# Tile 0 leaves the gating stage early, the last tile runs two chunks alone, and the weight stream waits for VectorE

## The chip, the cores and the metric

The kernel runs on one core of a Trainium2 chip. The metric is the device time of one execution, in microseconds (us). Before the change the median of three runs is 2240.0 us (2239.03 to 2240.32).

## The reference, cut to what matters

One step of a two-layer hybrid encoder runs over 1024 prompt rows and 32 sample rows of width 1024, all in fp32. Layer 0 mixes rows with spatial gating, layer 1 with trailing mean pooling. Each layer ends in a channel MLP with squared ReLU of width 4096. Conditioning (`mod`) is a product of a silu of `c` and a 1024 x 6144 weight per layer.

```python
mod = silu(c) @ w_ada[i] + b_ada[i]            # 6 vectors per request and layer
h = rmsnorm(x, g_norm[i, 0]) * (1 + sc1) + sh1
# layer 0: gating
z = gelu(h @ sgu_w_in); u, v = split(z, 2)
v = rmsnorm(v, g_v)                            # also an output, for the sample rows
s = einsum('gij,bnjgd->bnigd', w_s * mask, v) + b_s      # within chunks of 128 rows
mix = (u * s) @ sgu_w_out
# layer 1: mean over the last 2, 4, 8, 16 rows minus the row, a map per group, a scale
x = x + gt1 * rmsnorm(mix, g_norm[i, 1])
h = rmsnorm(x, g_norm[i, 2]) * (1 + sc2) + sh2
f = square(relu(h @ ffn_w_up[i])) @ ffn_w_down[i]
x = x + gt2 * rmsnorm(f, g_norm[i, 3])
```

## The kernel before

Activations lie transposed (features on partitions, rows on columns) in three token tiles: 384, 384 and 256 + 32 = 288 columns, called tiles 0, 1 and 2. To keep fp32 precision each operand of a large product is split in a high and a low part. `products` (L766) runs three matmuls per term: high x high (L771), low x high (L772) and high x low (L773).

**Weights.** Every weight arrives as pieces of 128 x 1024 fp32 (512 KB). SyncE's queue (SP) loads a piece into one of three `raw` buffers (L359), ScalarE (ACT) copies its high part `wh` (L367), and VectorE (DVE) subtracts to get the low part `wl`. Nearly all DVE work is recorded under line 79, so tiles tell it apart. Eight pairs of `wh` and `wl` are held at once. `w_finish` gives a pair back.

**One stream.** All loads stand in one list, `stream`, in a fixed order: weight pieces ("w"), conditioning pieces ("ada") and input rows ("x"). `weave` (L585) is called after each small unit of matmuls. It emits up to `streams` steps of the list (`stream_step`, L517) while a weight pair is free, and then pulls `fillers`, which are generators of residual, norm and output work, as long as a model of the time says that DVE is behind TensorE (`time["dve"] < time["pe"]`). `need_w` (L535) emits steps until the weight it is asked for is there. The order within each engine is thus fixed when the kernel is built.

**Conditioning.** From the v stage on, a conditioning piece is eight DVE operations on 128 x 256 each into an accumulator `aa` that has one buffer (`do_ada`, L429). Two pieces, so 16 operations, fill it. Then TensorE folds it with four small matmuls (`ada`, L453). After every fourth fold ACT copies the result (`adas`, L465) and TensorE transposes it (`adat`, L469). The folds go to a `deferred` list that the next step or `weave` empties.

**Stages of layer 0.** The v stage multiplies pieces p = 0..3 of `sgu_w_in` with nine row blocks (`v_mm`, L798 to L800; block 8, the sample rows, L790 and L791) and writes v to DRAM (`v_end`). The gating stage runs four pairs of groups, (0,1), (2,3), (4,5) and (6,7); for each pair `sgu_group` (L946) loads a 128 x 128 `w_s` per group and transposes it (`wsT`), and `sgu_item` (L958) then runs tiles 0, 1 and 2 in that order. An item has four "up" units (product `pu`, ACT Gelu L993, gating product `psp` L997, and DVE and ACT operations to `ush` and `usl`) and a "down" part (`po`), which is held back and emitted after the first up unit of the next item. After a tile's last item `mix_to_ffn` (L1138) becomes a filler: it takes the mixer's row norm (`pn_rs`, ACT reciprocal square root L675), adds the residual, takes the next norm (`pn_r`) and makes the FFN's input `hh` and `hl`.

**Passes.** The FFN runs as the list `passes` of (layer, chunk, tiles). A chunk is 512 of the 4096 hidden features and has eight weight pieces. In layer 0 chunks 0 and 1 run tile by tile, 2 and 3 over all three tiles, and 4 to 7 tile by tile; in layer 1 chunks 0 to 3 run tile by tile and 4 to 7 over all tiles. A pass over several tiles uses a loaded weight for all of them; a pass over one tile loads it again for the next.

**The end.** Tiles 0 and 1 go out through `to_out`, a filler: the final norm, 24 transposes `yT` (L1393), a copy `yo` (L1394) and a store (L1395) per tile. Tile 2 is last. While its final down products end, `scale_last` and `turn_last` (L1128, L1134) scale and transpose the result per feature block d. Then `last` (L1343) adds the squares, takes the norm per row (`pn_last`, `r_last`, then `ms_last`, `q_last`), applies it to the six 128 x 512 halves (`xlast`) and stores them (L1377).

Of the kernel before, what the change touches and what calls it, by code (L numbers as in the profile page):

```python
# [9 lines left out]
F32 = mybir.dt.float32  # L10
# [5 lines left out]
P = 128  # L16
D = 1024
# [17 lines left out]
def tile_stream_encoder_step(  # L35
# [84 lines left out]
    inv = const.tile([P, 16], F32, name="inv")  # L120
    epsT = const.tile([P, 1], F32, name="eps")
    nc.vector.memset(epsT, EPS * D / P)
    eps1 = const.tile([P, 1], F32, name="eps1")
    nc.vector.memset(eps1, EPS)
    for i in range(16):
        nc.vector.memset(inv[:, i : i + 1], 1.0 / (i + 1))

# [119 lines left out]
        for q in range(4):  # L247
            add_w(*v_item(p, q))

    def w_groups(gs):  # L250
        for g in gs:
            for k in range(2):
                f = 2 * g + k
                add_w(
                    ("u", g, k),
                    sgu_w_in[0][:, f * P : (f + 1) * P].rearrange("(k p) f -> p k f", p=P),
                    (8, P),
                )
        for q in range(2):
            for g in gs:  # L260
                add_w(
                    ("o", g, q),
                    sgu_w_out[0][g * 256 : (g + 1) * 256, q * 512 : (q + 1) * 512].rearrange(
                        "(k p) d -> p k d", p=P
                    ),
                    (2, 512),
                )
# [23 lines left out]
    passes += [(0, c, every) for c in range(2, 4)]  # L291
    passes += [(0, c, [t]) for t in every for c in range(4, 8)]
    passes += [(1, c, [t]) for t in every for c in range(4)]
    passes += [(1, c, every) for c in range(4, 8)]

    rest = []

# [20 lines left out]
        w_vpiece(p)  # L318
        some_ada(8)
    rest += [(1, j) for j in (*range(8, 16), *range(8), *range(16, 48))]  # L320
    groups = [(g, g + 1) for g in range(0, 8, 2)]
    for i, gs in enumerate(groups):
        w_groups(gs)
        if i < 3:
            some_ada((6, 8, 8)[i])
    wide = [n for n, (l, _, tiles) in enumerate(passes) if len(tiles) > 1]
    for n in range(len(passes)):
        w_chunk(n)
        if n in wide:
            some_ada(12 if passes[n][0] == 0 else 2)  # L330
    some_ada(99)

    worder = [s[1] for s in stream if s[0] == "w"]
# [1 line left out]
    wdone = set()  # L335
    raws = {}
    loads = {}
    state = {"issued": 0, "next": 0, "raw": 0}
    deferred = []

    def in_raw(k):
# [175 lines left out]
    def stream_step():  # L517
# [14 lines left out]
            state["raw"] -= 1  # L532
        issue()

    def need_w(key):  # L535
        while key not in witem:
            assert stream_ready(), key
            stream_step()
        return witem[key]
# [45 lines left out]
    def weave(streams=1):  # L585
        if streams:
            n = 0
            run_deferred()
            while n < streams and stream_ready():
                stream_step()  # L590
                n += 1
        while time["dve"] < time["pe"] and fillers:
            if not pull():
                break
# [27 lines left out]
    class Stat:  # L622

        def __init__(self, t, tag, split=True):
            self.t, self.tag, self.n, self.split = t, tag, ncol[t], split

        def square(self, k, src=None):

            if k == 0:
                self.sq = room("l", self.t, f"sq_{self.tag}")
            sq = self.sq
            w = 1 if src is None else 2
            act(
                out=sq[:, k, :] if w == 1 else sq[:, k : k + 2, :],
                in_=A(self.t, k) if w == 1 else src,
                func=AF.Square,
            )

            if w == 1:
                for j in [k - 1] if k < 7 else [6, 7]:
                    if j > 0:
                        tt(out=sq[:, 0, :], in0=sq[:, 0, :], in1=sq[:, j, :], op=ALU.add)
            else:
                for j in [k - 2] if k < 6 else [4, 6]:
                    if j > 0:
                        tt(out=sq[:, 0:2, :], in0=sq[:, 0:2, :], in1=sq[:, j : j + 2, :], op=ALU.add)
                if k == 6:
                    tt(out=sq[:, 0, :], in0=sq[:, 0, :], in1=sq[:, 1, :], op=ALU.add)  # L650
            if k + w == KB and self.split:
# [303 lines left out]
        nc.vector.memset(wt[64:P, 0:64], 0.0)  # L955
        return wt, bb

    def sgu_item(gs, t, mix, after):  # L958
        n = ncol[t]
        col0, npr, nsm = TILES[t]  # L960
        nch = npr // P
# [21 lines left out]
        def up(g, k):  # L983
            f = 2 * g + k
            if k == 0:
                inputs(g)
            vl, wr, bb = vls[g], wrs[g], mix[g][1]
            ps = ps_up(f"pu{g}_{t}_{k}")
            products(ps, n, up_terms(("u", g, k), t))
            if t == NT - 1:  # L990
                w_finish(("u", g, k))
            u = t_m(f"u{g}_{t}_{k}")
            act(out=u[:, :n], in_=ps[:, :n], func=AF.Gelu_apprx_tanh)  # L993
            sp = ps_up(f"psp{g}_{t}_{k}")
            tick(0.24 * nch + 0.2)
            for c in range(nch):
                mm(  # L997
                    sp[:, c * P : (c + 1) * P],
                    vl[:, c, k * P : (k + 1) * P],
                    wr[:, c * P : (c + 1) * P],  # L1000
                    start=True,
                    stop=True,
                )
# [29 lines left out]
            hid.append((a, b))  # L1033

        def down():
            for d in range(KB):
                ps = ps_dn(f"po{gs[0]}_{t}_{d}")
                terms = []
                for j, (a, b) in enumerate(hid):
                    wh, wl = need_w(("o", gs[j // 2], d // 4))  # L1040
                    o = (j % 2) * 512 + (d % 4) * P
                    terms.append((wh[:, o : o + P], wl[:, o : o + P], a[:, :n], b[:, :n]))
                products(ps, n, terms)
# [2 lines left out]
                    st = Stat(t, f"rs_{t}")  # L1046
                if after is not None:
                    st.square(d)
                if t == NT - 1 and d % 4 == 3:
                    for g in gs:  # L1050
                        w_finish(("o", g, d // 4))
                weave(d % 2)
            if after is not None:
                after(st)
# [8 lines left out]
    def ffn_item(p, t, after):  # L1063
# [17 lines left out]
        def down():  # L1081
            for d in range(KB):
# [11 lines left out]
                if after is not None:  # L1094
                    st.square(d)
                    if l == 1 and t == NT - 1:
                        scale_last(d)
                        if d > 0:
                            turn_last(d - 1)
                if last and d % 2 == 1:  # L1100
                    w_finish(("dn", p, d // 2))
# [59 lines left out]
    def to_ffn0(st):  # L1161
        fillers.append((f"ffn0_{st.t}", mix_to_ffn(st, 0)))

    for gs in groups:
        mix = {g: sgu_group(g) for g in gs}
        for t in range(NT):
            sgu_item(gs, t, mix, to_ffn0 if gs == groups[-1] else None)

    sgu_stack.close()
    late = pool("late")  # L1170
# [163 lines left out]
    def to_out(st):  # L1334
# [7 lines left out]

        def last():  # L1343

            turn_last(KB - 1)
            pn = ps_dn("pn_last")
            nb = len(LAST)
            for i, (c0, _, _) in enumerate(LAST):
                mm(
                    pn[:, 2 * i : 2 * i + 2],  # L1350
                    st.sq[:, 0, c0 : c0 + P],
                    ones[:, 0:2],
                    start=True,
                    stop=True,
                )
            sums = pn[:, : 2 * nb].rearrange("p (b c) -> p b c", c=2)[:, :, 0]
            ms, r, q = (t_st(f"{x}_last")[:, :nb] for x in ("ms", "r", "q"))
            act(out=r, in_=sums, func=AF.Abs_reciprocal_sqrt, bias=eps1, scale=1.0 / D)
            ts(ms, sums, 1.0 / D, EPS, op0=ALU.mult, op1=ALU.add)
            tt(out=q, in0=r, in1=r, op=ALU.mult)  # L1360
            stt(out=q, in0=q, scalar=-0.5, in1=ms, op0=ALU.mult, op1=ALU.mult)
            stt(out=r, in0=q, scalar=1.5, in1=r, op0=ALU.add, op1=ALU.mult)
            xt = last_ps["x"]
            dsts = [dst for _, _, dst in blocks]
# [82 lines left out]
```

## Time and profile before

| | |
|---|---|
| median of three runs | 2240.0 us |
| profiled execution: its own time | 2238.69 us |
| profiled execution: its span | 2236.9 us |
| TensorE busy | 98% |
| VectorE busy | 61% |
| ScalarE busy | 43% |
| 512 KB weight pieces of the FFN | 144 up, 144 down |
| conditioning pieces | 96 |

How to read the rows below. A row of the table by windows has the window, its length, the busy time and instruction count of TensorE (PE), its weight loads (PEld), DVE, ACT and GpSimd (POOL), then the TensorE clock that was granted (1.00 is full speed), the DMA engines' busy share and the GB/s. A row of the timeline has start, duration, engine, line, operation, output <- inputs, shapes, and in brackets the idle time before and what ended it. A row of the waits has the engine, what waited, what it waited for, then total us, times and longest. A group of the page has the line, operation and count, then busy time and mean ns of one. "SPq" is SyncE's DMA queue. Matmuls overlap, so a row's duration is longer than its spacing from the next.

### The profile page before, as it was taken

How to read it: one execution, taken by the hardware profiler on the slowest of the kernel's cores; microseconds unless marked ns; L12 is line 12 of the kernel's file. 1: busy time of each engine (PE TensorE's matmuls, PEld its weight loads, DVE VectorE, ACT ScalarE, POOL GpSimd, SP SyncE). 2: the span in 40 equal slices, each digit the busy share in tenths (PEclk: the TensorE clock that was granted, in tenths of full speed). 3: DMA queues.
4: the chain of work that ended last, by engine and by line, in shares of the span. 5: the costliest groups of instructions: out<-in, count | busy, mean ns of one | idle time of the engine just before them, and what ended most of it. 6: DMA issues, size and time to landing. Idle time of an engine off the chain costs nothing.

```text
span 2236.9 us, 33683 instructions
## 1 busy us (share of the span) xinstructions
PE 2197.3 (98%) x13478; PEld 2101.8 (94%) x13478; DVE 1371.4 (61%) x2609; ACT 957.5 (43%) x1645; POOL 0.7 (0%) x6
## 2 busy tenths in 40 slices
PE   7999799999999999999999999999999999999998
PEld 5777699999998999999999999999999999999998
DVE  4855735675568765766446869878765553424355
ACT  4633323121256654133435556666565542312334
POOL 0000000000000000000000000000000000000000
PEclk9999999999999999999999999999999999999998
DMA  8465613232235544333444546665454551202112
GB/s 298 149 226 164 206 53 116 79 126 88 78 104 184 171 132 142 104 123 109 132 125 131 166 156 201 184 189 163 145 166 135 152 155 45 93 10 85 57 50 95
DMA packets 344896, 295.67 MB, mean 132 GB/s; under 512 B 10178, under 2 KB 322954, under 8 KB 344740
## 3 DMA queue, kind: packets, MB, share of 16 engines
q1 hardware_dynamic: 344468, 293.43, 42.1%
q8 instruction: 105, 1.72, 0.3%
q14 instruction: 51, 0.42, 0.1%
q10 hardware_dynamic: 272, 0.10, 0.0%
HBM read 261.65 MB, written 31.84 MB: 131 GB/s over the span
## 4 chain that ended last, share of the span: by engine, by line
PE 91%; DMA 1%; DVE 1%; ACT 1%; issue 0%; DVEq 0%; SPq 0%; ACTq 0%
PE pf L771 11%; PE pf L772 11%; PE pf L773 11%; PE pg L771 11%; PE pg L772 11%; PE pg L773 11%; PE pu L771 3%; PE po L771 3%; PE po L772 3%; PE po L773 3%; PE pu L772 3%; PE pu L773 3%; PE pv L798 1%; PE pv L799 1%; PE pv L800 1%; PE pp L1310 1%
## 5 line engine op out<-in xcount | busy, mean ns | idle before, releaser
L771 PE MATMUL pf<-hh,wh_up 128*128 128x384 f32 (+1 forms) x1536 | 498.0, 324 | 1.2 <-ACT r L1075 1.0
L772 PE MATMUL pf<-hl,wh_up 128*128 128x384 f32 (+1 forms) x1536 | 497.0, 324 | 1.8 <-DVE hl L79 1.7
L771 PE MATMUL pg<-fh,wh_dn 128*128 128x384 f32 (+1 forms) x1536 | 498.3, 325 | 0.0
L773 PE MATMUL pf<-hh,wl_up 128*128 128x384 f32 (+1 forms) x1536 | 496.1, 323 | 0.0
L772 PE MATMUL pg<-fl,wh_dn 128*128 128x384 f32 (+1 forms) x1536 | 494.7, 322 | 0.0
L773 PE MATMUL pg<-fh,wl_dn 128*128 128x384 f32 (+1 forms) x1536 | 494.0, 322 | 0.0
L771 PEld LDWEIGHTS pf<-hh,wh_up 128*128 128x128 f32 x1536 | 288.6, 188 | 4.3 <-issue 2.0
L772 PEld LDWEIGHTS pf<-hl,wh_up 128*128 128x128 f32 x1536 | 288.7, 188 | 3.0 <-DVE hl L79 2.6
L771 PEld LDWEIGHTS pg<-fh,wh_dn 128*128 128x128 f32 x1536 | 288.4, 188 | 3.0 <-issue 1.2
L772 PEld LDWEIGHTS pg<-fl,wh_dn 128*128 128x128 f32 x1536 | 288.6, 188 | 0.7
L773 PEld LDWEIGHTS pg<-fh,wl_dn 128*128 128x128 f32 x1536 | 288.7, 188 | 0.0
L773 PEld LDWEIGHTS pf<-hh,wl_up 128*128 128x128 f32 x1536 | 288.6, 188 | 0.0
L367 ACT ACTIVATE wh_up<-raw 128x1024 fp32r<-128x1024 f32 x144 | 152.7, 1061 | 287.2 <-PE pf L772 230.8
L79 DVE TENSOR_TENSOR wl_up<-raw,wh_up 128x1024 fp32r<-128x1024 f32 x144 | 176.2, 1224 | 160.8 <-ACT wh_up L367 160.4
L79 DVE TENSOR_TENSOR acc<-acc,pg 128x384 f32<-128x384 f32 (+1 forms) x336 | 174.1, 519 | 159.8 <-PE pg L773 159.2
L367 ACT ACTIVATE wh_dn<-raw 128x1024 fp32r<-128x1024 f32 x144 | 152.7, 1061 | 206.2 <-PE pg L772 173.3
L79 DVE SCALAR_TENSOR_TENSOR aa<-raw,csil,aa 128x256 f32<-128x256 f32 x560 | 231.9, 478 | 2.4 <-DMA raw<-in_w_ada_dram 2.4
L79 DVE TENSOR_TENSOR wl_dn<-raw,wh_dn 128x1024 fp32r<-128x1024 f32 x144 | 176.2, 1224 | 86.4 <-ACT wh_dn L367 86.4
L1075 ACT ACTIVATE r<-pf 128x384 f32<-128x384 f32 (+1 forms) x192 | 86.6, 452 | 216.4 <-PE pf L773 211.6
L79 DVE TENSOR_TENSOR fl<-r,fh 128x384 fp32r<-128x384 f32 (+1 forms) x192 | 100.3, 523 | 115.0 <-ACT fh L925 113.6
L771 PE MATMUL pu<-hh,wh_u 128*128 128x384 f32 (+1 forms) x384 | 127.4, 332 | 0.9 <-DVE rv L874 0.9
L771 PE MATMUL po<-ush,wh_o 128*128 128x384 f32 (+1 forms) x384 | 125.6, 329 | 1.9 <-ACT ush L925 1.5
(254 smaller groups left out, 2904.2 us busy)
## 6 DMA issues: line engine op xcount, KB each, us to landing
raw<-in_ffn_w_up_dram SPq DMA_DIRECT2D x144, 512.0 KB, 4.1
raw<-in_ffn_w_down_dram SPq DMA_DIRECT2D x144, 512.0 KB, 3.4
raw<-in_w_ada_dram SPq DMA_DIRECT2D x96, 512.0 KB, 4.1
raw<-in_sgu_w_in_dram SPq DMA_DIRECT2D x32, 512.0 KB, 4.5
xd<-acc SPq DMA_DIRECT2D x8, 1536.0 KB, 7.4
xo_r<-xd SPq DMA_DIRECT2D x32, 384.0 KB, 3.7
vd<-vt SPq DMA_DIRECT2D x32, 256.0 KB, 2.9
raw<-in_sgu_w_out_dram SPq DMA_DIRECT2D x16, 512.0 KB, 3.8
```

Source lines behind the costliest of these rows:

```text
L79: return op(out, *args, **kw)
L367: act(out=wh, in_=r, func=AF.Copy)
L771: mm(ps[:, :n], wh, rh, start=i == 0, stop=False)
L772: mm(ps[:, :n], wh, rl, start=False, stop=False)
L773: mm(ps[:, :n], wl, rh, start=False, stop=i == last)
L798: mm(ps[:m, :], a_h, wh[:, o : o + 512], start=k == 0, stop=False)
L799: mm(ps[:m, :], a_h, wl[:, o : o + 512], start=False, stop=False)
L800: mm(ps[:m, :], a_l, wh[:, o : o + 512], start=False, stop=k == KB - 1)
L1075: act(out=r[:, :n], in_=ps[:, :n], func=AF.Relu)
L1310: mm(ps[:, :n], wg[:, k, e * P : (e + 1) * P], A(t, 2 * g + k), start=k == 0, stop=k == 1)
```

## The change

1. The last two pairs of groups run tile 0 first, then tiles 1 and 2 in a second round. The list `mixes` holds pairs with their tiles, and the weights carry the index of the mix. The weights, `w_s` and `b_s` of groups 4 to 7 are loaded twice.
2. In layer 1 chunks 6 and 7 run over tiles 0 and 1 first; then tile 2 runs its chunks 6 and 7 alone. Their weights are loaded twice.
3. `stream_waits` is new: `weave` takes no conditioning step while the model has DVE more than 0.5 us ahead of TensorE in work given out, and no weight that is more than five beyond the last one used while fillers are open and DVE is more than 1.0 us ahead. `need_w` is not bound by it. The conditioning pieces are laid out anew: 6 and 8 after the first two mixes (before 6, 8 and 8 after the first three), 12 after each of the layer 0 passes over three tiles as before, 4 after chunks 4 and 5 of tile 0 in layer 0 (new), and 4 after each of the layer 1 passes over several tiles (before 2).
4. In `last` the epsilon is added to the squares beforehand (`Stat.square`, at j == 1), the square of the last feature block is not added by DVE but summed by TensorE (six matmuls in place of three), and the chain of small DVE operations has three in place of four. `turn_last` runs in pairs at d = 2, 4, 6.

```diff
-    def w_groups(gs):
+    def w_groups(n):
+        gs, _ = mixes[n]
         for g in gs:
             for k in range(2):
                 f = 2 * g + k
                 add_w(
-                    ("u", g, k),
+                    ("u", n, g, k),
...
-    passes += [(1, c, every) for c in range(4, 8)]
+    passes += [(1, c, every) for c in range(4, 6)]
+
+    passes += [(1, c, every[:-1]) for c in (6, 7)]
+    passes += [(1, c, [NT - 1]) for c in (6, 7)]
...
-    groups = [(g, g + 1) for g in range(0, 8, 2)]
-    for i, gs in enumerate(groups):
-        w_groups(gs)
-        if i < 3:
-            some_ada((6, 8, 8)[i])
-    wide = [n for n, (l, _, tiles) in enumerate(passes) if len(tiles) > 1]
-    for n in range(len(passes)):
+
+    mixes = [((0, 1), every), ((2, 3), every), ((4, 5), every[:1]), ((6, 7), every[:1])]
+    mixes += [((4, 5), every[1:]), ((6, 7), every[1:])]
+    for n in range(len(mixes)):
+        w_groups(n)
+        if n < 2:
+            some_ada((6, 8)[n])
+    for n, (l, c, tiles) in enumerate(passes):
         w_chunk(n)
-        if n in wide:
-            some_ada(12 if passes[n][0] == 0 else 2)
+        if l == 0:
+            some_ada(12 if len(tiles) > 1 else 4 if c in (4, 5) and tiles == every[:1] else 0)
+        elif len(tiles) > 1:
+            some_ada(4)
     some_ada(99)
...
+    def stream_waits():
+
+        kind, key = stream[state["next"]][:2]
+        if kind == "w":
+            return bool(fillers) and wpos[key] > state["used"] + 5 and time["dve"] > time["pe"] + 1.0
+        return kind == "ada" and time["dve"] > time["pe"] + 0.5
+
     def need_w(key):
+        state["used"] = max(state["used"], wpos[key])
...
-            while n < streams and stream_ready():
+            while n < streams and stream_ready() and not stream_waits():
...
-                for j in [k - 1] if k < 7 else [6, 7]:
-                    if j > 0:
+                for j in [k - 1] if k < 7 else [6, 7] if self.split else [6]:
+                    if j == 1 and not self.split:
+                        stt(
+                            out=sq[:, 0, :],
+                            in0=sq[:, 0, :],
+                            scalar=epsT,
+                            in1=sq[:, j, :],
+                            op0=ALU.add,
+                            op1=ALU.add,
+                        )
+                    elif j > 0:
                         tt(out=sq[:, 0, :], in0=sq[:, 0, :], in1=sq[:, j, :], op=ALU.add)
...
-                        if d > 0:
+                        if d in (2, 4, 6):
+                            turn_last(d - 2)
                             turn_last(d - 1)
...
-    for gs in groups:
+    for p, (gs, tiles) in enumerate(mixes):
         mix = {g: sgu_group(g) for g in gs}
-        for t in range(NT):
-            sgu_item(gs, t, mix, to_ffn0 if gs == groups[-1] else None)
+        for t in tiles:
+            sgu_item(p, t, mix, to_ffn0 if gs[-1] == 7 else None)
...
-            turn_last(KB - 1)
+            turn_last(KB - 2)
             pn = ps_dn("pn_last")
             nb = len(LAST)
-            for i, (c0, _, _) in enumerate(LAST):
-                mm(
-                    pn[:, 2 * i : 2 * i + 2],
-                    st.sq[:, 0, c0 : c0 + P],
-                    ones[:, 0:2],
-                    start=True,
-                    stop=True,
-                )
+            for k in (0, KB - 1):
+                if k > 0:
+                    turn_last(KB - 1)
+                for i, (c0, _, _) in enumerate(LAST):
+                    mm(
+                        pn[:, 2 * i : 2 * i + 2],
+                        st.sq[:, k, c0 : c0 + P],
+                        ones[:, 0:2],
+                        start=k == 0 and i == 0,
+                        stop=k > 0 and i == nb - 1,
+                        skip_group_check=True,
+                    )
...
-            act(out=r, in_=sums, func=AF.Abs_reciprocal_sqrt, bias=eps1, scale=1.0 / D)
-            ts(ms, sums, 1.0 / D, EPS, op0=ALU.mult, op1=ALU.add)
+            act(out=r, in_=sums, func=AF.Abs_reciprocal_sqrt, scale=1.0 / D)
             tt(out=q, in0=r, in1=r, op=ALU.mult)
-            stt(out=q, in0=q, scalar=-0.5, in1=ms, op0=ALU.mult, op1=ALU.mult)
+            stt(out=q, in0=sums, scalar=-0.5 / D, in1=q, op0=ALU.mult, op1=ALU.mult)
             stt(out=r, in0=q, scalar=1.5, in1=r, op0=ALU.add, op1=ALU.mult)
```

More of the change, by code (lines that the diff above doesn't have):

```diff
@@ L122, in tile_stream_encoder_step @@
     nc.vector.memset(epsT, EPS * D / P)
-    eps1 = const.tile([P, 1], F32, name="eps1")
-    nc.vector.memset(eps1, EPS)
     for i in range(16):
@@ L261, in w_groups @@
                 add_w(
-                    ("o", g, q),
+                    ("o", n, g, q),
                     sgu_w_out[0][g * 256 : (g + 1) * 256, q * 512 : (q + 1) * 512].rearrange(
@@ L337, in tile_stream_encoder_step @@
     loads = {}
-    state = {"issued": 0, "next": 0, "raw": 0}
+    state = {"issued": 0, "next": 0, "raw": 0, "used": 0}
     deferred = []
@@ L956, in sgu_group, with sgu_item @@
         return wt, bb
-    def sgu_item(gs, t, mix, after):
+    def sgu_item(p, t, mix, after):
+        gs, tiles = mixes[p]
+        last = t == tiles[-1]
         n = ncol[t]
@@ L988, in up @@
             ps = ps_up(f"pu{g}_{t}_{k}")
-            products(ps, n, up_terms(("u", g, k), t))
-            if t == NT - 1:
-                w_finish(("u", g, k))
+            products(ps, n, up_terms(("u", p, g, k), t))
+            if last:
+                w_finish(("u", p, g, k))
             u = t_m(f"u{g}_{t}_{k}")
@@ L1039, in down @@
                 for j, (a, b) in enumerate(hid):
-                    wh, wl = need_w(("o", gs[j // 2], d // 4))
+                    wh, wl = need_w(("o", p, gs[j // 2], d // 4))
                     o = (j % 2) * 512 + (d % 4) * P
@@ L1048, in down @@
                     st.square(d)
-                if t == NT - 1 and d % 4 == 3:
+                if last and d % 4 == 3:
                     for g in gs:
-                        w_finish(("o", g, d // 4))
+                        w_finish(("o", p, g, d // 4))
                 weave(d % 2)
@@ L1343, in last @@
         def last():
-            turn_last(KB - 1)
+            turn_last(KB - 2)
             pn = ps_dn("pn_last")
             nb = len(LAST)
-            for i, (c0, _, _) in enumerate(LAST):
-                mm(
-                    pn[:, 2 * i : 2 * i + 2],
-                    st.sq[:, 0, c0 : c0 + P],
-                    ones[:, 0:2],
-                    start=True,
-                    stop=True,
-                )
+            for k in (0, KB - 1):
[10 more added lines that the diff above has]
+                    )
             sums = pn[:, : 2 * nb].rearrange("p (b c) -> p b c", c=2)[:, :, 0]
-            ms, r, q = (t_st(f"{x}_last")[:, :nb] for x in ("ms", "r", "q"))
-            act(out=r, in_=sums, func=AF.Abs_reciprocal_sqrt, bias=eps1, scale=1.0 / D)
-            ts(ms, sums, 1.0 / D, EPS, op0=ALU.mult, op1=ALU.add)
+            r, q = (t_st(f"{x}_last")[:, :nb] for x in ("r", "q"))
+            act(out=r, in_=sums, func=AF.Abs_reciprocal_sqrt, scale=1.0 / D)
             tt(out=q, in0=r, in1=r, op=ALU.mult)
-            stt(out=q, in0=q, scalar=-0.5, in1=ms, op0=ALU.mult, op1=ALU.mult)
+            stt(out=q, in0=sums, scalar=-0.5 / D, in1=q, op0=ALU.mult, op1=ALU.mult)
             stt(out=r, in0=q, scalar=1.5, in1=r, op0=ALU.add, op1=ALU.mult)
```

## The prediction

> **What bounds the kernel now.** I began with the page's first lines, went on to the table by windows to find where TensorE is not busy or not at full clock, then to TensorE's waits for what it stood on there, and last to the timeline at those places.
>
> ```profile
> span 2236.9 us, 33683 instructions
> PE 2197.3 (98%) x13478; PEld 2101.8 (94%) x13478; DVE 1371.4 (61%) x2609; ACT 957.5 (43%) x1645; POOL 0.7 (0%) x6
> ```
>
> TensorE bounds the kernel. At 98% busy, only a change of its work or of its few pauses can move the time. The windows show where the pauses are:
>
> ```profile
> 0.00:56.00 56.00, 44.10 (x280) 29.02 (x284) 27.88 (x93) 26.80 (x46) 0.70 (x6) 0.97 0.88 297
> ...
> 126.00:236.00 110.00, 109.93 (x522) 84.22 (x520) 59.76 (x148) 39.90 (x75) 0.00 (x0) 1.00 0.60 196
> 236.00:280.00 44.00, 32.39 (x177) 27.93 (x177) 36.64 (x83) 16.89 (x27) 0.00 (x0) 0.88 0.76 233
> 280.00:656.00 376.00, 376.00 (x2409) 366.95 (x2409) 217.04 (x490) 94.62 (x165) 0.00 (x0) 1.00 0.30 92
> 656.00:700.00 44.00, 38.36 (x224) 35.34 (x223) 34.21 (x66) 28.44 (x45) 0.00 (x0) 0.92 0.40 118
> 700.00:1560.00 860.00, 860.00 (x5316) 845.22 (x5315) 601.05 (x1003) 437.04 (x720) 0.00 (x0) 1.00 0.49 151
> ...
> 2200.00:2236.90 36.90, 28.30 (x192) 26.37 (x191) 20.93 (x42) 16.46 (x40) 0.00 (x0) 0.81 0.24 86
> ...
> 1792.00:1848.00 56.00, 56.00 (x414) 56.00 (x413) 31.59 (x45) 27.44 (x41) 0.00 (x0) 1.00 0.50 152
> ```
>
> There are four places: the start (11.9 us idle, not touched by the change), 236 to 280 (11.6 us idle: end of the v stage and first items of gating), 656 to 700 (5.64 us idle: last gating item into the FFN), and the tail. Between them TensorE is full, also in a stretch of one-tile FFN passes (1792 to 1848, 56.00 of 56). The waits name what is late:
>
> ```profile
> PE psp L997 <- DMA vl<-vd: 5.0, 1, 5.0
> PE ada L453 <- DVE aa L79: 4.6, 1, 4.6
> PE yT L1393 <- DVE xlast L79: 1.8, 1, 1.8
> PE pf L772 <- DVE hl L79: 1.7, 1, 1.7
> PE po L771 <- ACT ush L925: 1.5, 1, 1.5
> ```
>
> The first two lie in 236 to 280: DVE works off conditioning pieces in one run, and loads queue behind them. The pf and po waits lie in 656 to 700.
>
> **Part 1: tile 0 leaves the gating stage early.** Before, the norms of tile 0, the last gating items and the FFN's first products come together:
>
> ```profile
> 660.11 1.28 ACT L675 ACT_TABLE_LOAD   x1
> ...
> 660.80 1.05 PE L997 MATMUL psp<-wr,vl 128*128 128x128 f32 x4 [0.58 <-DVE wr L79]
> ...
> 661.41 0.49 ACT L675 ACTIVATE r_r_0x<-pn_r_0x 128x384 f32<-128x384 f32 x1
> ...
> 663.97 1.28 ACT L675 ACT_TABLE_LOAD   x1
> ...
> 685.53 0.44 PE L772 MATMUL pf<-hl,wh_up 128*128 128x384 f32 x1 [1.69 <-DVE hl L79]
> ```
>
> ACT changes function tables between Gelu and reciprocal square root, 1.28 us each time, while po waits for `ush`; 22 us later the FFN's product waits for its input `hl`. Each pause is followed by a halved clock:
>
> ```profile
> 664.00:666.00 2.00, 2.00 (x10) 2.00 (x10) 0.45 (x1) 1.99 (x3) 0.00 (x0) 0.50 0.71 245
> ...
> 684.00:686.00 2.00, 0.47 (x3) 0.47 (x4) 2.00 (x5) 0.89 (x2) 0.00 (x0) 1.00 0.43 129
> ...
> 688.00:690.00 2.00, 2.00 (x8) 2.00 (x8) 2.00 (x5) 1.24 (x2) 0.00 (x0) 0.50 0.05 14
> ```
>
> So this stage loses 5.64 us of pause, and by its mean clock of 0.92 another 0.08 x 38.4 = 3.1 us: 8.7 us. In the changed order of instructions tile 0's residual and norms are worked off among the items of tiles 1 and 2, about four items before the FFN's first product; that product's 24 matmuls then stand in one piece, with nothing of `hl` between, and the two table changes are no longer back to back. There are as many table loads as before. One short wait stays, where a norm's result is taken next to a `psp`: as a remainder I take 1.0 us, between none and half of the old 8.7. The four additional `wsT` transposes go on TensorE, at the spacing of the first stage's transposes:
>
> ```profile
> 45.16 2.04 PE L500 MATMUL xT<-ident,raw 128*128 128x128 f32 x16
> ```
>
> 2.04 / 16 = 0.13 us, so 0.5 us for four. **Part 1: -8.7 + 1.0 + 0.5 = -7.2 us, from -8.7 to -4.**
>
> [...]
>
> **The weights loaded again.** 16 more in gating and 16 more in layer 1's chunks 6 and 7, each with these prices:
>
> ```profile
> L367 ACT ACTIVATE wh_up<-raw 128x1024 fp32r<-128x1024 f32 x144 | 152.7, 1061 | 287.2 <-PE pf L772 230.8
> L79 DVE TENSOR_TENSOR wl_up<-raw,wh_up 128x1024 fp32r<-128x1024 f32 x144 | 176.2, 1224 | 160.8 <-ACT wh_up L367 160.4
> ...
> raw<-in_ffn_w_up_dram SPq DMA_DIRECT2D x144, 512.0 KB, 4.1
> ```
>
> In all 32 x 1.22 = 39 us of DVE, 34 us of ACT and 16 MB of loads. In gating DVE is busy 217 of 376 us, and the eight conditioning pieces that now come later free 64 operations at 0.40 us (row at 110.23 below), 26 us, against 16 x 1.22 = 20 us put in. In the one-tile passes at 1792 DVE is at 56% and DMA at 0.50 while TensorE never pauses. I count them at nothing; the cover is this slack, and without it the price is in the rival below. The conditioning pieces moved to layer 0's chunks 4 and 5, eight of 3.2 us, lie where DVE is at 601 of 860 us. SP also issues four more `ws` and four more `bs` loads, which are small.
>
> **Part 2: tile 2 alone, and the new tail.**
>
> ```profile
> 2220.64 0.49 PE L1134 MATMUL yT<-ident,acc 128*128 128x128 f32 x3
> ...
> 2221.81 0.46 DVE L79 TENSOR_TENSOR sq_rf<-sq_rf 128x288 f32<-128x288 f32 x1 [0.51 <-ACT sq_rf L635]
> ...
> 2223.19 0.26 ACT L1358 ACTIVATE r_last<-pn_last,eps 128x3 f32<-128x3 f32 x1 [0.66 <-PE pn_last L1349]
> ...
> 2224.14 4.19 DVE L79 SCALAR_TENSOR_TENSOR xlast<-yT,r_last,xlast 128x512 f32<-128x512 f32 x6
> ...
> 2233.02 1.17 SPq L1377 DMA_DIRECT2D out_dram<-xlast  x2
> ```
>
> The last down product ends at 2220.64; call this L. The span ends at L + 16.26. Of that, `xlast` ends at 2228.33 (L + 7.69), but its last two stores are issued only at 2233.02, behind tile 1's transposes, copies and stores on SP, and end the span 2.71 us after their issue (2236.9 less 2234.19). After the change tile 1 is out before, so those stores are bound by DVE alone. DVE's add of the last square starts at 2221.81, so the square itself is there at about L + 1.1, and the add (0.46) is not needed any more; I put `r_last` 0.6 us earlier than before, ending at L + 2.2, three DVE operations of 0.2 to L + 2.75, six `xlast` of 0.70 to L + 6.95, and one issue (0.4) and landing (2.7) to L + 10.05. That is 6.2 us less behind L. But tile 1's 24 output transposes, part of which filled this tail, now run before L: 24 x 0.13 = 3.1 us on TensorE. For its waits at the new place I allow 0.3. **Part 2: -6.2 + 3.1 + 0.3 = -2.8 us, from -4 to -1.5.**
>
> **Part 3: the stream waits for VectorE.** `stream_waits` stops nothing on the chip; it changes the order. Two places matter. In 236 to 280 the order of the conditioning pieces and of the v loads behind them is the same as before on all engines, since there the model has DVE behind TensorE: the stall of 11.6 us stays, at 0. In the v stage it acts early: conditioning steps are held back, and the stream is two steps behind when v piece 2 begins. Before:
>
> ```profile
> 108.06 0.39 PE L790 MATMUL pv<-wh_v,hs 128*64 128x512 f32 x1
> 108.29 0.39 PE L791 MATMUL pv<-wl_v,hs 128*64 128x512 f32 x1
> ...
> 110.23 5.62 DVE L79 SCALAR_TENSOR_TENSOR aa<-raw,csil,aa 128x256 f32<-128x256 f32 x14
> ...
> 120.16 0.42 PE L453 MATMUL ada<-aa,pick 128*32 128x128 f32 x8
> ...
> 120.82 1.06 ACT L367 ACTIVATE wh_v<-raw 128x1024 fp32r<-128x1024 f32 x1 [4.69 <-DMA raw<-in_sgu_w_in_dram]
> ...
> 122.59 0.33 PE L469 MATMUL adat<-ident,adas 128*128 128x128 f32 x1 [0.88 <-ACT adas L465]
> 127.95 1.22 DVE L79 TENSOR_TENSOR wl_v<-raw,wh_v 128x1024 fp32r<-128x1024 f32 x1
> ```
>
> Before, the weights of piece 2 are made from 121 on, while piece 1 still runs, and 126 to 236 has no pause (109.93 of 110). After, the fold of one conditioning accumulator comes at the end of block 7 of piece 1 (call it T), and only then is `aa` free for the next 16 operations: T + 0.5 + 16 x 0.41 = T + 7.1, or 7.6 with issue and landing of the piece. On TensorE behind T stand the fold (0.42), the 16 matmuls of block 8 at 0.23 (3.7) and a transpose: it comes to the fold of that accumulator, which stands ahead of most of piece 2's block 0, near T + 5. So it waits 2.1 to 2.6. Then `wl` of piece 2's first weight, 1.22 us, stands behind the 16 operations on DVE: another 0.5 to 0.9; the next weights, issued one by one as `raw` frees, add about 1. Together 4.3, less the old stage's pause of 0.88 that the new order may keep or lose (I take off 0.6): **Part 3: +3.7 us, from +2 to +5.5**, the upper end with the clock halved behind it for 2 to 4 us, as at 664 and 688.
>
> **The sum.** -7.2 - 2.8 + 3.7 = -6.3 us. It is made against the profiled execution, 2238.69 us (1.79 above its span): 2232.4. The median of the runs shown, 2240.0, is 1.31 above that execution, so on it the forecast is **2233.7 us**.
>
> **Rivals.** (a) *No net change.* Gating's end is cured by half only: the short norm wait also halves the clock (as at 664, 2 us at 0.50 lose 1.0) and Part 3 costs its upper end: -4 + 5.5 - 1.5 = 0, so 2240. For it speaks that behind the wait of 0.58 us at 660 the clock is at 0.50 four us later; against it, that the norms now have some four items between them and their users. (b) *Slower: the reloaded weights come late.* At each of the four switches to weights loaded again, the first would arrive a full lead late: 4.1 (load) + 1.06 (`wh`) + 1.22 (`wl`) = 6.4 us, four times 25.5, so 2240.0 - 6.3 + 25.5 = 2259. It decides where the stream is less than 6.4 us ahead of its use, which the held back weights (no more than five ahead) bring nearer. Against it: one-tile passes run at 56.00 of 56 now, and five pieces are five times 24 matmuls at 0.135 (56 / 414), 16 us. (c) *The change cures what its wait is for:* the stall in 236 to 280 goes too; with 11.6 us off, 2222. Against it stands the unchanged order there. [...]
>
> **How the numbers follow.** Forecast 0.62, (a) 0.17, (b) 0.12, (c) 0.05, (d) 0.04. A measurement of this kernel can tell about 0.2%, 4.5 us: faster is below 2235.5, slower above 2244.5. The forecast's own bounds run from -8.7 - 4 + 2 = -10.7 to -4 - 1.5 + 5.5 = 0, so 2229 to 2240; I give 0.59 of its 0.62 to times below 2235.5. Faster: 0.59 + 0.05 = 0.64. Within: 0.03 + 0.17 + 0.04 = 0.24. Slower: 0.12. The range 2228.5 to 2241 holds the forecast, (a) and (d), 0.83 less a little at its lower edge.
>
> **What would show it.** Right: no wait of `pf` for `hl` and a clock near 1.00 at the end of gating; a wait of `ada` for `aa` of 2 to 3 us near 140 in the v stage, which was not there; the waits 5.0 and 4.6 in 236 to 280 as before; the last down product some 10 us ahead of the end; TensorE full in the gating items of tiles 1 and 2 and in tile 2's last passes. Wrong: TensorE waiting for `wl_u`, `wl_o`, `wl_up` or `wl_dn` at the switches (b), a v stage without a pause or with over 6 us of it, or a stall at 264 to 276 that is gone.

## The result, and the profile after

| | before | changed |
|---|---|---|
| median | 2239.6 us (2238.24 to 2240.32) | 2232.0 us (2231.47 to 2233.09) |
| span of the profiled execution | 2236.9 us | 2230.0 us |

The ratio is 0.9967, with a 95% interval of 0.9955 to 0.9979: 7.4 us faster (4.7 to 10.1). The forecast was 6.3 us.

The page's first lines, and windows that answer to those shown of before (the same columns):

```profile
span 2230.0 us, 33872 instructions
...
PE 2193.8 (98%) x13488; PEld 2099.9 (94%) x13488; DVE 1404.9 (63%) x2646; ACT 989.9 (44%) x1677; POOL 0.7 (0%) x6
```

```profile
126.00:160.00 34.00, 30.94 (x143) 22.26 (x143) 21.22 (x49) 11.68 (x22) 0.00 (x0) 0.95 0.61 201
236.00:290.00 54.00, 43.11 (x237) 36.98 (x236) 41.73 (x99) 20.74 (x32) 0.00 (x0) 0.91 0.68 208
656.00:700.00 44.00, 44.00 (x292) 43.52 (x291) 37.49 (x65) 29.68 (x48) 0.00 (x0) 1.00 0.61 189
```

The end of the gating stage (656 to 700) is full and at full clock: 292 matmuls in the 44 us that held 224 before. A pause has come into the v stage (126 to 160), which had none. The stall after 236 is there as before.

TensorE's waits in the changed kernel:

```profile
PE ada L458 <- DVE aa L79: 6.9, 3, 4.5
...
PE psp L1022 <- DMA vl<-vd: 4.3, 1, 4.3
...
PE pf L796 <- DVE wl_up L79: 0.6, 1, 0.6
```

The waits of `po` for `ush` and of `pf` for `hl` are gone. `ada` waits 2.3 us more than before, and `pf` now waits for `wl_up`, which was not among the waits of before.

**Where the time went, by starts.** The windows count a matmul's modelled length as busy, 0.34 us for 384 columns where the next one starts 0.173 us later, so a pause shows about 0.17 us too short; and a slow product looks like work (in 688 to 690 before, at a granted clock of 0.50, one lasts 0.52 us and the next starts 0.32 us later). For every kernel I therefore took the starts of TensorE's matmuls from the timeline and added up how much later than usual each next one began. Usual is the spacing in the full stretches: 0.173 us after 384 columns, 0.132 after 288, 0.229 after 512. Some 2 us in every 40 of the gating stage are the gating product's own slower spacing: six `psp` of 128 columns take 0.80 us from the first start to the start behind them (304.33 to 305.13, before), 0.133 each. From its starts, against the usual spacing per column, I estimate 1.7 to 3.0 us per 40 in 300 to 660 before, and 1.1 to 2.6 in the changed kernel. The last column is the time from the end of the last down product (read as the start of the transpose behind it) to the end of the span.

| kernel | v stage (118 to 240) | first gating items (240 to 300) | gating's end (640 to 760) | layer 0's FFN from 760 | behind the last product |
|---|---|---|---|---|---|
| before | 3.4 | 15.7 | 13.7 | 3.7 | 16.3 |
| changed | 6.7 | 16.1 | 2.2 | 6.1 | 9.9 |
| mix_only | 4.1 | 16.4 | 2.2 | 5.6 | 15.9 |
| last_only | 3.8 | 16.5 | 11.9 | 4.0 | 14.7 |
| split_only | 2.6 | 17.0 | 12.5 | 3.4 | 10.3 |
| tail_only | 3.6 | 16.5 | 12.3 | 4.0 | 9.8 |
| no_wait | 4.1 | 16.7 | 2.2 | 6.7 | 10.5 |
| even_ada | 4.6 | 16.7 | 2.2 | 3.9 | 9.9 |
| no_burst | 3.2 | 15.6 | 2.3 | 4.0 | 10.1 |
| no_burst_6 | 8.2 | 13.8 | 2.3 | 4.0 | 10.3 |
| before_state | 3.9 | 5.0 | 11.4 | 3.3 | 15.8 |
| changed_state | 7.7 | 5.6 | 2.3 | 6.0 | 9.8 |
| state_late | 3.8 | 5.1 | 2.3 | 3.7 | 10.0 |

The kernels are those of the experiments below. From one profile to the next the same stage differs by up to 1.8 us: the four kernels with the old gating and the filler in its old place (before, last_only, split_only, tail_only) show 11.9 to 13.7 at the gating's end.

The tail in the changed kernel's timeline:

```profile
2220.12 0.49 PE L1160 MATMUL yT<-ident,acc 128*128 128x128 f32 x3
...
2222.17 0.17 ACT L1388 ACTIVATE r_last<-pn_last 128x3 f32<-128x3 f32 x1 [0.17 <-PE pn_last L1378]
...
2223.04 4.19 DVE L79 SCALAR_TENSOR_TENSOR xlast<-yT,r_last,xlast 128x512 f32<-128x512 f32 x6
2223.82 3.77 SPq L1406 DMA_DIRECT2D out_dram<-xlast  x6
```

The last product ends at 2220.12; `r_last` ends 2.2 us later, `xlast` 7.1 us later, and all six stores go out as `xlast` comes, with nothing of tile 1 between.

### The profile page after: what moved, and what is told of

Read it like the earlier page. It is cut to its first block, busy times and chain, and to the rows that moved or that the text cites. A ratio compares the mean times of both kernels' runs of the same rounds, so it can differ in the third digit from the quotient of the medians.

```text
span 2230.0 us, 33872 instructions
## 1 busy us (share of the span) xinstructions
PE 2193.8 (98%) x13488; PEld 2099.9 (94%) x13488; DVE 1404.9 (63%) x2646; ACT 989.9 (44%) x1677; POOL 0.7 (0%) x6
## 4 chain that ended last, share of the span: by engine, by line
PE 92%; DMA 3%; DVE 2%; ACT 2%; issue 0%; SPq 0%; DVEq 0%; ACTq 0%
PE pf L794 11%; PE pf L795 11%; PE pf L796 11%; PE pg L794 11%; PE pg L795 11%; PE pg L796 11%; PE po L794 3%; PE pu L794 3%; PE po L796 3%; PE po L795 3%; PE pu L796 3%; PE pu L795 3%; PE pv L821 2%; PE pv L822 2%; PE pv L823 2%; PE psp L1022 1%
## 5 line engine op out<-in xcount | busy, mean ns | idle before, releaser
L79 DVE TENSOR_TENSOR wl_up<-raw,wh_up 128x1024 fp32r<-128x1024 f32 x152 | 185.6, 1222 | 167.5 <-ACT wh_up L372 167.4
L372 ACT ACTIVATE wh_up<-raw 128x1024 fp32r<-128x1024 f32 x152 | 161.0, 1059 | 276.9 <-PE pf L795 201.0
L372 ACT ACTIVATE wh_dn<-raw 128x1024 fp32r<-128x1024 f32 x152 | 160.9, 1059 | 207.7 <-PE pg L795 159.3
L79 DVE TENSOR_TENSOR wl_dn<-raw,wh_dn 128x1024 fp32r<-128x1024 f32 x152 | 185.8, 1222 | 92.2 <-ACT wh_dn L372 91.9
```

What stands on the lines that cost most here:

```text
L79: return op(out, *args, **kw)
L372: act(out=wh, in_=r, func=AF.Copy)
```

## The experiments

Each was timed in several rounds beside the kernel before, whose medians in the three sets were 2239.05, 2239.67 and 2240.44 us.

### Part 1 alone: mix_only

```diff
-    groups = [(g, g + 1) for g in range(0, 8, 2)]
+    mixes = [((0, 1), every), ((2, 3), every), ((4, 5), every[:1]), ((6, 7), every[:1])]
+    mixes += [((4, 5), every[1:]), ((6, 7), every[1:])]
...
+        if l == 0:
+            some_ada(12 if len(tiles) > 1 else 4 if c in (4, 5) and tiles == every[:1] else 0)
+        elif len(tiles) > 1:
+            some_ada(2)
```

> The kernel before with part 1 alone (tile 0 first in the last two pairs of groups, and the conditioning pieces of the gating stage laid out as in the change). No waits, passes and end as before. Theory: the end of the gating stage gives back all that the start-to-start times of TensorE's matmuls show as lost there, about 11.4 us, less 0.5 for four transposes: 2239.6 - 10.9 = 2228.7. Rival: the blind term of -7.2, from idle time and mean clock: 2232.4. A second rival, that the change needs the waits to work and the pause moves to the items of tiles 1 and 2: 2236 or above.

Measured: 2233.3 us, ratio 0.9976 (0.9966 to 0.9986), so 5.4 us less (3.1 to 7.6). The end of gating gave back what the theory said (13.7 to 2.2), so the pause did not move to the items of tiles 1 and 2. But layer 0's FFN lost 1.9 us more than before, a cost that the expectation had not counted. 11.5 - 1.9 - 0.5 leaves 9 us, 1.5 more than the interval's upper end. Part of this rest may be the one profile of before: counted from last_only's 11.9 the stage gives back 9.7, and 9.7 - 1.9 - 0.5 = 7.3 lies inside the interval. The profiled execution (2231.29) also lies 2 us under the median. The rest isn't explained further.

### Part 2, and its halves: tail_only, last_only, split_only

```diff
-    passes += [(1, c, every) for c in range(4, 8)]
+    passes += [(1, c, every) for c in range(4, 6)]
+    passes += [(1, c, every[:-1]) for c in (6, 7)]
+    passes += [(1, c, [NT - 1]) for c in (6, 7)]
```

This diff alone is split_only; the changes of `last`, `Stat.square` and `turn_last` alone are last_only; both are tail_only.

> The kernel before with part 2 alone (tile 2 runs chunks 6 and 7 of layer 1 by itself, and the new norm at the end). Theory: 6.4 us less behind the last down product, 3.1 us of tile 1's transposes moved ahead of it: -3.0 to -3.3, so 2236.4. Rival: the weights loaded again for tile 2 come late, which loses one lead of 6.4 us: 2243. Second rival: the copies and transposes of tile 1 hold up tile 2's products, and nothing is won: 2239.6.

> The kernel before with the new end alone (squares of the last block summed by TensorE, epsilon added beforehand, three small DVE operations in place of four, transposes in pairs); passes as before. Theory: tile 1's transposes, copies and stores still stand ahead of the last stores on SP's queue, and they set the end, so the shorter norm chain is hidden: 2239.6 - 0.3, between 2238.9 and 2239.8. Rival: the norm chain sets the end (`r_last` 0.6 us earlier, `xlast` with it) and all the rest follows it: 2239.6 - 1.0 = 2238.6 or below.

> The kernel before with tile 2's chunks 6 and 7 of layer 1 run alone, and the old end. Theory: the last stores are then bound by the norm chain and by `xlast` on DVE; without the new end it is 0.5 us for the add on DVE and 0.2 to 0.6 us for the chain longer than with it: the last down product to the end takes 10.6 to 11.0 us in place of 9.9, and the time is 2236.3 against 2235.5 with both. Rival: the new end is hidden here too: 9.9 us and 2235.5.

Measured: tail_only 2235.5 us, ratio 0.9984 (0.9976 to 0.9993); last_only 2238.8 us, 0.9998 (0.9989 to 1.0007); split_only 2236.2 us, 0.9987 (0.9978 to 0.9995). Part 2 is worth 3.6 us (1.6 to 5.4), as expected, and the reloaded weights are not late: among the waits of tail_only there is none for a weight of the FFN. Most of it is the split: by its ratio split_only gives 2.9 us. The new end has no effect that these times can tell. The profiles differ, though: with the new end and old passes the span ends 14.7 us behind the last product in place of 16.3, so my reason that tile 1's stores hide it fell. The stores do go out earlier:

```profile
2222.51 4.19 DVE L79 SCALAR_TENSOR_TENSOR xlast<-yT,r_last,xlast 128x512 f32<-128x512 f32 x6
...
2230.51 1.19 SPq L1388 DMA_DIRECT2D out_dram<-xlast  x2
```

That timeline is of last_only, where the last product ends at 2219.58: `xlast` starts 2.9 us behind it (3.5 before) and the last stores are issued 10.9 us behind it (12.4 before). Tile 1's transposes wait for `xlast` to free their accumulators (2.0 us here, 1.8 before), so they move with it.

### The waits of the stream taken out: no_wait

```diff
-            while n < streams and stream_ready() and not stream_waits():
+            while n < streams and stream_ready():
```

> The changed kernel with the waits of the stream taken out of `weave`; the mixes, passes, layout of conditioning pieces and the end stay. Theory: the waits cause both new pauses of the changed kernel, the one for `aa` in the v stage (3.1 us idle and 1.5 us of clock at 140 to 160, against 1.3 us before) and the one for `wl_up` at 1109 (1.2 us idle, 2.5 us with the products that it spreads). Then both go: 2232.0 - 3.5 - 2.5 = 2226. First rival: the pause at 1109 comes from the conditioning pieces moved into layer 0's chunks 4 and 5, not from a weight held back; it stays, and the time is 2228.5. Second rival: the waits do what they are for elsewhere, and without them conditioning pieces hold up TensorE in the gating stage: 2232 or above.

Measured: 2227.8 us, ratio 0.9956 (0.9944 to 0.9969). Against their own runs of before, the changed kernel is 0.9967 and this one 0.9956: the difference is 2.5 us, though the intervals overlap (the medians are 4.2 us apart). By starts the v stage falls from 6.7 to 4.1, which is the waits' price in the profile, and the first rival is right about the other pause: it stays. So the second rival fell too: with the waits gone nothing new holds up TensorE in gating.

### The pause at 1100: even_ada

```diff
-            some_ada(12 if len(tiles) > 1 else 4 if c in (4, 5) and tiles == every[:1] else 0)
+            some_ada(12 if len(tiles) > 1 else 2 if c >= 4 and tiles == every[:1] else 0)
```

The base is no_wait. Its timeline shows the queue of SP, DVE's work on the conditioning pieces, and then the product that waits for its weight:

```profile
1089.65 10.02 SPq L364 DMA_DIRECT2D raw<-in_w_ada_dram  x4
...
1097.60 4.84 DVE L79 SCALAR_TENSOR_TENSOR aa<-raw,csil,aa 128x256 f32<-128x256 f32 x12
...
1102.47 6.90 SPq L364 DMA_DIRECT2D raw<-in_ffn_w_up_dram  x2
...
1107.76 0.44 PE L794 MATMUL pf<-hh,wh_up 128*128 128x384 f32 x1 [0.81 <-ACT wh_up L372]
```

Four conditioning loads take 10 us of SP's queue, since a `raw` buffer must come free for each, and DVE frees it when it has worked the piece off (in all of no_wait the loads into `raw` wait 264.2 us for the operations on `aa`, in 75 waits). Its twelve operations end at 1102.44, the next weight's load is issued at 1102.47, and its `wh` is there only at 1107.7, when TensorE is already waiting.

> The changed kernel without the waits of the stream, and with the eight conditioning pieces of layer 0's chunks 4 and 5 of tile 0 laid two each after its chunks 4, 5, 6 and 7. Theory: the pause of `pf` for `wh_up` and `wl_up` near 1100 (2.7 us spread over the products, in every kernel with that layout) comes from four pieces in a row on the one queue and the three raw buffers ahead of one-tile weights; with two at a time it goes, 2227.8 - 2.7 = 2225.1. Rival: DVE as a whole is short there, or the reloaded weights are, and the pause moves to the next passes: 2227.8.

Measured: 2225.0 us, ratio 0.9933 (0.992 to 0.9947), 2.8 us less than no_wait by the medians (5.2 by the ratios, whose intervals just overlap). By starts the stage falls from 6.7 to 3.9, as before, so the pause did not move to the next passes. The windows of no_wait and of even_ada, from 1080 to 1120:

```profile
1080.00:1120.00 40.00, 38.28 (x227) 36.65 (x227) 30.06 (x59) 15.31 (x22) 0.00 (x0) 1.00 0.59 178
```

```profile
1080.00:1120.00 40.00, 40.00 (x237) 39.56 (x236) 24.90 (x41) 16.14 (x22) 0.00 (x0) 1.00 0.51 157
```

### The stall after 236: no_burst, no_burst_6, and then the filler

The prediction had put this stall, the largest of all, down to conditioning pieces in a row on DVE. So they were taken away from there (even_ada as the base):

```diff
-        if n < 2:
-            some_ada((6, 8)[n])
+        some_ada((0, 6, 0, 0, 0, 0)[n])
...
-            some_ada(12 if len(tiles) > 1 else 2 if c >= 4 and tiles == every[:1] else 0)
+            some_ada(12 if len(tiles) > 1 else 2 if c >= 4 and tiles[0] < 2 else 0)
```

In no_burst_6 the second mix has eight, and the last v piece six in place of eight.

> As the run with even pieces, and also without the six conditioning pieces behind the first mix (after the second mix six, in layer 0's chunks 4 to 7 two each for tiles 0 and 1, so that their sum is the same). Theory: the stall of 13 us at 240 to 280 is those pieces, which occupy DVE and whose loads stand on SP ahead of the loads of v (`vl`) until DVE frees a raw buffer. Without them it goes but for the usual 2: 2225.1 - 11 = 2214. Rival: the loads of v wait for the stores of v or for the v stage's norm, whatever stands between; then 5 us of it stay: 2220. Second rival: the pieces make a pause wherever they go, 2225.

> As the run without the burst, with six conditioning pieces in place of eight behind the last v piece, and eight behind the second mix. Theory: the same 2214, less up to 1 us since DVE has 6 us less to do at the end of the v stage and the first mix's weights come earlier. Rival: the fold that is then open over the first mix, or the weights ahead of the norms of v on DVE, cost what this gives: 2214 to 2216.

Measured: 2240.0 us, ratio 1.0003 (0.9995 to 1.0012), and 2243.0 us, 1.0013 (1.0004 to 1.0022). The theory fell. The stall is 15.6 where it was 16.7, and only the names in the waits are others. The timeline of no_burst there:

```profile
268.65 0.74 DVE L79 SCALAR_TENSOR_TENSOR vst<-vst,rv,gvb 32x512 f32<-32x512 f32 x1 [2.58 <-DMA gvb<-in_sgu_g_v_dram]
271.71 0.48 PE L974 MATMUL wsT<-ident,ws 128*128 128x128 f32 x1 [3.83 <-DMA ws<-in_sgu_w_s_dram]
```

DVE waits for a load there, and so does TensorE, each for a small one. What the kernels with the stall have in common is in SP's queue, here of no_wait:

```profile
257.96 0.34 SPq L932 DMA_DIRECT2D out_dram<-vst  x1
...
264.08 0.33 SPq L932 DMA_DIRECT2D out_dram<-vst  x1
...
268.82 0.33 SPq L932 DMA_DIRECT2D out_dram<-vst  x1
269.24 0.37 SPq L921 DMA_DIRECT2D gvb<-in_sgu_g_v_dram  x1
270.80 0.39 SPq L364 DMA_DIRECT2D raw<-in_w_ada_dram  x1
272.47 0.38 SPq L993 DMA_DIRECT2D vl<-vd  x1
```

The filler `sgu_state` makes the output of the normalised v rows of the sample: four rounds of two loads (`vst`, `gvb`), one DVE product and a store. Each store stands on SP until its round is through, 4.7 to 6.1 us from one to the next, and `vl`, which the next product needs, stands behind; `vst`, `gvb` and `vl` also share three buffers. Both show in SP's own waits in the kernel before, from 244 to 285: 6.6 us ahead of the filler's stores, and 2.9 us in which loads of `vst` and `vl` wait for a store to land. The experiments below take both away together, so how they share the stall stays open.

The new places of the conditioning pieces cost some 18 us in the profiled execution (15 by the medians), at the border of the layers. The windows of no_burst and of even_ada from 1360 to 1480:

```profile
1360.00:1480.00 120.00, 111.14 (x705) 104.52 (x704) 104.75 (x162) 79.61 (x136) 0.00 (x0) 0.94 0.56 175
```

```profile
1360.00:1480.00 120.00, 120.00 (x830) 118.91 (x829) 100.03 (x147) 75.88 (x126) 0.00 (x0) 1.00 0.58 177
```

By starts this stretch loses 20.3 us in place of 2.3. With the pieces given to tile 1's passes too, DVE has 105 us of work in 120 there, against 100, and among TensorE's waits of no_burst `pf` stands with its input. That the pieces on DVE make this input late is argued, and no run shows it:

```profile
PE pf L793 <- ACT hh L767: 4.4, 1, 4.4
```

The next experiments move the filler alone: in state_late from even_ada, in changed_state from the changed kernel, in before_state from the kernel before.

```diff
-    fillers.append(("state", sgu_state()))
...
+    fillers.append(("state", sgu_state()))
+
     sgu_stack.close()
```

> The kernel with even pieces (no waits of the stream, two conditioning pieces each in layer 0's chunks 4 to 7), and the filler that makes the sample rows' v output (four rounds of `vst`, `gvb`, one DVE product and a store) appended behind the last mix in place of ahead of the first. Theory: the stall of 13 us at 240 to 280 is that filler. Its stores stand on SP until its loads have come and DVE has multiplied, its tiles take the three buffers that `vl` uses too, and `vl`, `ws` and the conditioning loads stand behind. Without it the usual 2 to 3 us per 40 us are left: 2225.0 - 11.5 = 2213.5. Rival: the six conditioning pieces behind the first mix are enough for a stall of their own on DVE: half stays, 2219. Second rival: the filler makes the same stall where it goes, at the start of the FFN: 2225.

> The changed kernel as it is, with only that filler moved behind the last mix. Theory: the same 11.5 us less: 2232.0 - 11.5 = 2220.5; the waits of the stream do not matter for it. Rival: with the waits the conditioning pieces come later and meet the filler: above 2224.

> The kernel before with only that filler moved behind the last mix. Theory: 11.5 us less at 240 to 280, but the filler then runs where the end of the gating stage and the first FFN pass already meet with 11 us lost there, on SP ahead of the FFN's weights: between 2228 and 2232. Rival: that stage gets worse by as much: 2239.

Measured: state_late 2212.8 us, ratio 0.9879 (0.9864 to 0.9894); changed_state 2219.7 us, 0.991 (0.9897 to 0.9924); before_state 2228.3 us, 0.9947 (0.9934 to 0.9959). All three are as the theory said: the stall falls from 16 to 5, in the kernel before too, and the filler makes no new one. With the six conditioning pieces still in place, TensorE is busy for 62.25 of 64 us. Windows of the changed kernel and of state_late:

```profile
236.00:300.00 64.00, 53.11 (x296) 46.98 (x295) 43.46 (x102) 24.10 (x39) 0.00 (x0) 0.92 0.57 176
```

```profile
236.00:300.00 64.00, 62.25 (x367) 58.32 (x368) 38.55 (x91) 24.02 (x41) 0.00 (x0) 1.00 0.48 152
...
640.00:720.00 80.00, 80.00 (x498) 79.52 (x498) 70.97 (x125) 57.76 (x94) 0.00 (x0) 1.00 0.63 194
```

state_late is the fastest of all: 27 us below the kernel before and about 19 below the changed one.

## Why the prediction was right

The forecast held: -6.3 us, measured -7.4, and the three parts act where it said. That the sum came so close is partly luck: part 1 gave back more than its term, and a cost that was counted at nothing took some of it away. Several steps were off in size or in reason.

- **Part 1, -7.2.** The mechanism was right, the size too small. The start-to-start count gives 13.7 before and 2.2 after, 11.5 us, less 0.5 for four transposes. Two terms failed. "5.64 us of pause" and "3.1 us" of clock add up to 8.7, while starts in the same window, 656 to 700, lose 12.4 before and 1.9 after: the busy time covers a matmul's tail in each pause (about 0.17 us) and part of each slow product (0.52 us where starts lie 0.32 apart). And the remainder of 1.0 us that I left standing did not appear. The range, whose lower end was -8.7, did not hold it, not even counted from last_only's 11.9 (9.7 less 0.5).
- **The reading behind part 1's clock term.** "Each pause is followed by a halved clock" holds for two of the four longer pauses of that stage, those at 660 and 685 (0.50 in 664 to 666 and in 688 to 690). The two others left the clock at 1.00. One of them is the wait of `po` for `ush`, which lies at 672, and not beside the table changes of 660 and 664, where `psp` waited for `wr`:

```profile
672.49 0.67 PE L771 MATMUL po<-ush,wh_o 128*128 128x288 f32 x3 [1.54 <-ACT ush L925]
...
696.09 0.45 PE L771 MATMUL pf<-hh,wh_up 128*128 128x384 f32 x1 [1.01 <-ACT r L1075]
```

```profile
674.00:676.00 2.00, 1.76 (x14) 1.72 (x14) 2.00 (x6) 1.57 (x3) 0.00 (x0) 1.00 0.32 112
...
696.00:698.00 2.00, 1.91 (x11) 1.91 (x12) 2.00 (x3) 2.00 (x7) 0.00 (x0) 1.00 0.10 30
```

  The mean of 0.92 that the term was taken from stands all the same.
- **The conditioning pieces moved to chunks 4 and 5, counted at nothing.** The cover I named was DVE's slack over the whole stretch, and that was there: 9.9 of 40 us in no_wait at 1080 to 1120. What went wrong was the order: four pieces in a row held SP's queue and the three `raw` buffers until DVE had worked them off, and a one-tile weight came late: 2 to 3 us, which even_ada gave back. Rival (b) had named a late weight, but at the switches to reloaded weights, and there none came late.
- **Part 2, -2.8.** Right in kind and size: the end came 9.9 us behind the last product where 10.05 was worked out, and tail_only measured 3.6 less. What the parts of it gave was not worked out: it is mostly the split, and the new end's share can't be told from nothing.
- **Part 3, +3.7.** Right, though its terms add up to anything from 3.6 to 4.5 where it took 4.3 before the deduction of 0.6: the v stage lost 3.3 us more, with the wait of `ada` for `aa` at the place that the order gave (2.19 us of 2.1 to 2.6):

```profile
143.84 1.66 DVE L79 SCALAR_TENSOR_TENSOR aa<-raw,csil,aa 128x256 f32<-128x256 f32 x4
...
145.15 0.41 PE L458 MATMUL ada<-aa,pick 128*32 128x128 f32 x4 [2.19 <-DVE aa L79]
...
147.28 0.63 PE L823 MATMUL pv<-wh_v,hl 128*128 128x512 f32 x1
147.70 0.63 PE L821 MATMUL pv<-wh_v,hh 128*128 128x512 f32 x1
```

  Behind it the products start 0.42 us apart in place of 0.23, at a granted clock of 0.56 and 0.59 (146 to 148, 148 to 150). That the waits are the cause is shown by no_wait, where the stage falls back to 4.1.
- **The stall in 236 to 280, left at 0.** It did stay, so rival (c) fell, but the reason in the reading was wrong: "DVE works off conditioning pieces in one run, and loads queue behind them". The table of waits names only what ended each wait; moving the filler of small loads and stores ended the stall, and taking the conditioning pieces away did not.
- Rival (a) asked for the gating pauses to be half cured, and they went wholly. For (d), with 0.04 of the chances, no run shows a ground; in 656 to 700, where the pauses are gone in the changed kernel, the granted clock is 1.00 in place of 0.92.

## What to carry to other kernels

Here, where the order within engines is fixed, small loads and stores that wait for each other on one DMA queue were dear: four rounds of 32 rows held TensorE up by some 11 us (16.1 by starts with them, 5.6 without, changed and changed_state), and the table of waits named DVE and a load for it. To see such a stall, read the queue's own order ahead of the late load, and take away one suspect at a time; without the pieces that the waits named the stall stayed at 15.6 us. Size a pause by the starts of the instructions around it and not by idle time alone, and count a moved load by how long it holds its buffer and the queue, and not only by the share of time that the engine has to spare.

## What the runs showed of the hardware

The granted clock fell to half after some short pauses: to 0.50 in 664 to 666 after a wait of 0.58 us and in 688 to 690 after one of 1.69 us (before), and to 0.56 and 0.59 in 146 to 150 after one of 2.19 us (changed). After others that were as long it stayed at 1.00: after 1.54 us at 672.49 and 1.01 us at 696.09 (before), and after two close together, 0.81 us at 1107.76 and 0.64 us between 1108 and 1112 in no_wait, whose windows from 1104 to 1112 are at 1.00. So the length of the wait alone does not decide it here, and what does isn't settled by these runs.
